# Token-major last down-projection: split weights begin 128 bytes further on in their tile, and the three widened products of a group stand apart

## The chip, the core and the metric

The kernel runs on one core of one Trainium2 chip. The metric is the device time of one execution in microseconds (us); three runs give a median. A profile is one execution with the hardware profiler on; TensorE's granted clock was 0.999 of full speed in it.

## What is computed

A decoder trunk of two layers over 272 tokens (16 learned meta tokens ahead of 256 tokens of input), model width 2048, 16 heads of 128, feed-forward width 8192. Layer 0 is forgetting attention with a squared-ReLU MLP; layer 1 is stick-breaking attention on a shared K and V with a second MLP. The part that the change touches is the end of it:

```python
def squared_relu_mlp(h, w_up, w_down):
    u = h @ w_up
    return jnp.square(jax.nn.relu(u)) @ w_down
...
        h = h + squared_relu_mlp(rms_norm(h, norm_mlp[layer]), w_up[layer], w_down[layer])
    return rms_norm(h, final_norm)[:, N_META:]
```

All values are float32.

## The kernel before

**Products in three.** [...] So each operand is split into a high part and the rest (`hi`, `lo`): ScalarE copies the raw values into the high part, VectorE subtracts it from the raw values. Each product of two matrices becomes three matmuls: hi by hi, lo by hi, hi by lo. Every matmul has its own load of the 128 x 128 stationary operand; the other operand moves through the array, one column per token or per weight.

**Feature-major stages.** Nearly all stages keep the residual stream with features on the partitions and tokens along the row. `gemm_group` (L188) makes 512 output features: the weights are stationary, 128 x 128 at a time, and `x` moves, 272 columns wide in layer 0, 256 columns in layer 1 from its query projection on (`t0` = M = 16, which leaves the meta tokens out), 272 again in the shared K and V. A group has four blocks `kb` of 512 input features, each in two halves (`hf`) of two chunks of 128 (`kc`). One half is a transfer of 512 KB into `raw` on SyncE's queue, one copy on ScalarE (L235) and one subtraction on VectorE (L236), into tiles `whi` and `wlo` that each have four buffers. With `t0` = 0 a chunk's three matmuls stand in a row (L258); with `t0` = 16 the part of the product is the outer loop (L256), so that all hi-by-hi products of a run come first. `gemm_matmul` (L175; its matmul is L177 in the profile) pins the order of the products on TensorE.

**Where operands begin.** A tile of split weights has rows of two chunks, each 576 floats (2304 bytes) wide, of which 512 are used. With `t0` = 16 these begin at float 16 of 576, 64 bytes behind the chunk's beginning; with `t0` = 0 the chunks lie packed, 512 floats each, from 0 on. The tiles of `x` (`Split`, L105) have 16 rows of 640 floats (2560 bytes); `ROWS` places the two parts in a row: `hi` at float 48 and `lo` at 368 with `t0` = 0 (192 and 1472 bytes), at 0 and 320 with `t0` = 16 (0 and 1280 bytes). The pool of the split weights and that of the `x` tiles are opened one behind the other, and all these tiles are whole multiples of 256 bytes long.

**Widened products.** In some groups with `t0` = 16 a few products take `SPAN` = 6 columns more than the 256 that are needed (262). The six columns go into the part of the accumulator's bank that nobody reads. `widen` names the chunks for which the product of the group's first 128 outputs is widened, in each of its three parts.

**The last quarter.** The last of the four down-projections of layer 1 (`last_down`, L835) runs token-major: tokens are on the partitions of the result, so that the final norm and the output need no transpose. Here `x` (the tile `x_u`) is stationary, 128 tokens `b` at a time, and the split weights move, 256 columns `h` at a time. `load_split` (L269) fetches and splits a block as above (L275, L283, L284); `token_products` (L288, its matmul is L293) issues for each entry `(kc, b, h)` of an order the three matmuls in a row, and `behind` (L183) pins each one behind the last. Four groups `g` of 512 outputs have 4 blocks x 4 chunks x 2 x 2 x 3 = 192 matmuls each, 768 in all. In groups 0 to 2, blocks 0 to 2 go through the order kc, b, h, and block 3 finishes one accumulator after the other, each followed by `add_rows` (L799). In group 3 tokens `b` = 0 go through all blocks first (96 matmuls) and `finish_rows` (L813) sends them out, while `b` = 1 goes through the same weights a second time; so all four blocks must be kept, and blocks 1 and 2 lie in `home`, a tile in an `x` buffer with the same rows of 576 floats. The split weights' 512 floats begin at float 16 here too (L282). With `widen` set, the three matmuls of the group's first entry (block 0, chunk 0, b = h = 0) are 262 columns wide (L291).

Of the kernel before, what the change touches and what calls it, by code (L numbers as in the profile page):

```python
# [27 lines left out]
SPAN = 6  # L28
# [8 lines left out]
def yoco_kernel(ctx: ExitStack, tc: tile.TileContext, hT_in, gains, b_f, w_f, w_qkv0, w_o0, w_up, w_dn,  # L37
# [145 lines left out]
    def behind(ins):  # L183

        tc.add_manual_dep(ins.ins, queued[0].name, mybir.DependencyInfo(mybir.DependencyClass.NoSync,
                                                                        mybir.DependencyReason.DATA))
# [82 lines left out]
    def load_split(wblk, kb, label, home=None):  # L269

        src_w = wblk[kb].rearrange("p (k c) -> p k c", k=4)
        parts = []
        for hf in range(2):
            raw = wraw.tile([P, 2, 512], F32, tag="raw", name=f"raw_{label}_{kb}_{hf}")
            nc.sync.dma_start(raw, src_w[:, 2 * hf:2 * hf + 2])  # L275
            if home is None:
                hi = wspl.tile([P, 2 * 576], F32R, tag="whi", name=f"whi_{label}_{kb}_{hf}").rearrange(
                    "p (k c) -> p k c", k=2)
                lo = wspl.tile([P, 2, 576], F32R, tag="wlo", name=f"wlo_{label}_{kb}_{hf}")
            else:  # L280
                hi, lo = home[:, hf, 0], home[:, hf, 1]
            hi, lo = hi[:, :, 16:528], lo[:, :, 16:528]  # L282
            nc.scalar.activation(hi, raw, AF.Copy)  # L283
            nc.vector.tensor_tensor(out=lo, in0=raw, in1=hi.bitcast(F32), op=ALU.subtract)  # L284
            parts.append((hi, lo))
        return parts

    def token_products(accs, sp, parts, kb, order, widen=False):  # L288

        for kc, b, h in order:  # L290
            over = SPAN if widen and kb == kc == b == h == 0 else 0  # L291
            for w, x in ((0, sp.hi), (1, sp.hi), (0, sp.lo)):
                ins = nc.tensor.matmul(accs[b][h][:, :256 + over], x[:, 4 * kb + kc, b * P:(b + 1) * P],  # L293
                                       parts[kc // 2][w][:, kc % 2, 256 * h:256 * h + 256 + over],
                                       start=kb == kc == w == 0 and x is sp.hi, stop=kb == kc == 3 and x is sp.lo)
                behind(ins)
                queued[:] = [ins.ins]
# [243 lines left out]
    for g in range(4):  # L541
# [44 lines left out]
        for j in range(4):  # L586
            h = 4 * g + j
# [247 lines left out]
    def last_down(f, u):  # L835
# [3 lines left out]
        for g in range(4):  # L839
            pool, tag = ((patt, "patt"), (pacc, "acc"))[g % 2]  # L840
            accs = [[pool.tile([P, 512], F32, tag=tag, name=f"acc_t{g}_{b}_{h}") for h in range(2)] for b in range(2)]
            parts = []
            for kb in range(4):
                parts.append(load_split(w_dn[1, f, g], kb, f"t{g}", home[:, kb - 1] if g == 3 and kb in (1, 2) else None))
                if g == 3:
                    token_products(accs, u, parts[kb], kb, [(kc, 0, h) for kc in range(4) for h in range(2)], True)
                elif kb < 3:
                    token_products(accs, u, parts[kb], kb, [(kc, b, h) for kc in range(4) for b in range(2)
                                                            for h in range(2)], True)
                else:  # L850
                    for b in range(2):
                        for h in range(2):
                            token_products(accs, u, parts[kb], kb, [(kc, b, h) for kc in range(4)])
                            add_rows(g, b, h, accs[b][h])
# [68 lines left out]
```

## Time and profile before

| What | us |
| --- | --- |
| median of three runs | 2263.16 |
| lowest and highest of them | 2263.07, 2263.64 |
| profiled execution | 2263.8 |
| its span (first to last instruction) | 2262.1 |
| around the span | 1.7 |
| last quarter on TensorE (L293), first to last start | 2163.8 to 2254.2 |

PE is TensorE's matmuls, PEld its weight loads, DVE VectorE, ACT ScalarE, POOL GpSimd, SP SyncE. A row of one line's instructions has the tiles (out<-in), the count, the least, median and greatest time of one in ns, the first and last start in us, and the shapes. A matmul's time is longer than the distance to the next one, because matmuls are pipelined; the pace of a stretch is the distance of its first and last start over the count less one. Rows of the timeline have start, duration and what is done; neighbouring instructions with the same tiles are merged, with their count and the shape of the first.

### The profile page before, as it was taken

How to read it: one execution, taken by the hardware profiler on the slowest of the kernel's cores; microseconds unless marked ns; L12 is line 12 of the kernel's file. 1: busy time of each engine (PE TensorE's matmuls, PEld its weight loads, DVE VectorE, ACT ScalarE, POOL GpSimd, SP SyncE). 2: the span in 40 equal slices, each digit the busy share in tenths (PEclk: the TensorE clock that was granted, in tenths of full speed). 3: DMA queues.
4: the chain of work that ended last, by engine and by line, in shares of the span. 5: the costliest groups of instructions: out<-in, count | busy, mean ns of one | idle time of the engine just before them, and what ended most of it. 6: DMA issues, size and time to landing. Idle time of an engine off the chain costs nothing.

```text
span 2262.1 us, 44965 instructions
## 1 busy us (share of the span) xinstructions
PE 2253.3 (100%) x18845; PEld 2251.0 (100%) x18845; DVE 1390.2 (61%) x1997; ACT 1125.4 (50%) x1577; POOL 114.8 (5%) x220
## 2 busy tenths in 40 slices
PE   9999999999999999999999999999999999999998
PEld 9999999999999999999999999999999999999998
DVE  7877786554455455455566688876555555555654
ACT  6664565453354344344454577755544443543543
POOL 1000000000000000000000011100000000001421
PEclk9999999999999999999999999999999999999999
DMA  7545545555555555555555544565655656556564
GB/s 248 184 153 178 184 161 169 186 169 185 179 176 182 174 177 185 173 184 177 170 192 183 179 163 159 172 202 186 201 188 190 205 187 201 189 190 204 188 193 144
DMA packets 116507, 413.37 MB, mean 183 GB/s; under 512 B 13456, under 2 KB 15776, under 8 KB 116304
## 3 DMA queue, kind: packets, MB, share of 16 engines
q1 hardware_dynamic: 113904, 406.25, 55.1%
q10 hardware_dynamic: 2000, 3.03, 0.5%
q8 instruction: 147, 2.41, 0.4%
q0 software_dynamic: 400, 1.21, 0.1%
q14 instruction: 56, 0.46, 0.1%
HBM read 408.33 MB, written 2.11 MB: 181 GB/s over the span
## 4 chain that ended last, share of the span: by engine, by line
PE 100%; DVE 0%; ACT 0%; issue 0%; DVEq 0%
PE acc L177 93%; PE acc_t L293 4%; PE ps L400 1%; PE po L495 1%; PE ps L398 0%; PE po L498 0%; PE idle L68 0%; PE pf L344 0%; PE pc L486 0%; PE pom L641 0%; PE ps L605 0%; DVE hrow L832 0%; DVE hrow L830 0%; PE pf_sum L351 0%; DVE hrow L803 0%; DVE sqr L806 0%
## 5 line engine op out<-in xcount | busy, mean ns | idle before, releaser
L236 DVE TENSOR_TENSOR wlo<-raw,whi 128x1024 fp32r<-128x1024 f32 (+1 forms) x742 | 890.7, 1217 | 604.4 <-ACT whi L235 598.1
L235 ACT ACTIVATE whi<-raw 128x1024 fp32r<-128x1024 f32 (+1 forms) x742 | 764.3, 1050 | 881.8 <-PE acc L177 850.6
L177 PE MATMUL acc<-x_m,whi 128*128 128x272 f32 (+1 forms) x4096 | 642.6, 281 | 0.0
L177 PE MATMUL acc<-x_u,whi 128*128 128x272 f32 (+1 forms) x3584 | 576.7, 282 | 0.0
L177 PEld LDWEIGHTS acc<-x_m,whi 128*128 128x128 f32 x4096 | 565.6, 188 | 0.0
L177 PEld LDWEIGHTS acc<-x_u,whi 128*128 128x128 f32 x3584 | 504.0, 188 | 0.0
L177 PE MATMUL acc<-x_m,wlo 128*128 128x272 f32 (+1 forms) x2048 | 441.0, 281 | 0.0
L177 PE MATMUL acc<-x_u,wlo 128*128 128x272 f32 (+1 forms) x1792 | 404.1, 282 | 0.0
L177 PE MATMUL acc<-x_a,whi 128*128 128x272 f32 (+1 forms) x2048 | 352.9, 286 | 0.0
L177 PEld LDWEIGHTS acc<-x_m,wlo 128*128 128x128 f32 x2048 | 323.3, 188 | 0.0
L177 PEld LDWEIGHTS acc<-x_a,whi 128*128 128x128 f32 x2048 | 300.5, 189 | 0.9 <-issue 0.5
L177 PEld LDWEIGHTS acc<-x_u,wlo 128*128 128x128 f32 x1792 | 290.7, 188 | 0.0
L177 PE MATMUL acc<-x_a,wlo 128*128 128x272 f32 (+1 forms) x1024 | 252.8, 285 | 0.0
L177 PE MATMUL acc<-x_kv,whi 128*128 128x272 f32 x1024 | 192.4, 287 | 0.0
L177 PEld LDWEIGHTS acc<-x_a,wlo 128*128 128x128 f32 x1024 | 175.7, 189 | 0.0
L177 PE MATMUL acc<-x_o,whi 128*128 128x272 f32 (+2 forms) x1024 | 161.9, 282 | 0.0
L177 PEld LDWEIGHTS acc<-x_kv,whi 128*128 128x128 f32 x1024 | 160.2, 188 | 0.0
L177 PE MATMUL acc<-x_kv,wlo 128*128 128x272 f32 x512 | 147.2, 288 | 0.0
L177 PEld LDWEIGHTS acc<-x_o,whi 128*128 128x128 f32 x1024 | 141.8, 188 | 0.0
L177 PE MATMUL acc<-x_o,wlo 128*128 128x272 f32 (+1 forms) x512 | 110.3, 282 | 0.0
L300 DVE TENSOR_TENSOR rows<-acc,rows 128x272 f32<-128x272 f32 (+1 forms) x144 | 62.2, 432 | 74.2 <-PE acc L177 74.2
L177 PEld LDWEIGHTS acc<-x_kv,wlo 128*128 128x128 f32 x512 | 96.5, 188 | 0.0
(216 smaller groups left out, 1529.2 us busy)
## 6 DMA issues: line engine op xcount, KB each, us to landing
raw<-w_up SPq DMA_DIRECT2D x256, 512.0 KB, 3.8
raw<-w_dn SPq DMA_DIRECT2D x224, 512.0 KB, 3.7
raw<-w_qkv SPq DMA_DIRECT2D x92, 512.0 KB, 4.0
raw<-w_o SPq DMA_DIRECT2D x64, 512.0 KB, 4.3
raw<-w_kv SPq DMA_DIRECT2D x64, 512.0 KB, 3.7
raw<-w_q SPq DMA_DIRECT2D x32, 512.0 KB, 4.4
raw_t<-w_dn SPq DMA_DIRECT2D x32, 512.0 KB, 4.3
fk<-f_dram ACTq DMA_DIRECT2D x4, 544.0 KB, 7.9
```

The source lines that it names most:

```text
L177: ins = nc.tensor.matmul(*args, **kw).ins
L235: on_act = nc.scalar.activation(hp, src, AF.Copy)
L236: on_dve = nc.vector.tensor_tensor(out=lp, in0=src, in1=hp.bitcast(F32), op=ALU.subtract)
L293: ins = nc.tensor.matmul(accs[b][h][:, :256 + over], x[:, 4 * kb + kc, b * P:(b + 1) * P], parts[kc // 2][w][:, kc % 2, 256 * h:256 * h + ...
L300: nc.vector.tensor_tensor(out=hT[:, c, t0:], in0=acc, in1=hT[:, c, t0:], op=ALU.add)
L400: nc.tensor.matmul(ps[:, 144:416], qs[a][:, j, :], ks[b][:, j, :], start=i == 0, stop=i == 2)
L495: ins = nc.tensor.matmul(po[:, i, :], vk, pk, start=i == k == 0, stop=False)
```

## The change

Two edits. In `load_split` the 512 used floats of each chunk begin at float 48 instead of 16 of 576, that is 192 instead of 64 bytes behind the chunk's beginning; this holds for `whi`, `wlo` and `home`, and for what ScalarE and VectorE write and TensorE reads. In `token_products` the widened products of a group are no longer the three matmuls of the first entry, but the first matmul (hi by hi) of the entries 0, 2 and 4 of block 0's order: the 1st, the 7th and the 13th. In groups 0 to 2 these are chunk 0 with b = 0, chunk 0 with b = 1 and chunk 1 with b = 0; in group 3 they are chunks 0, 1 and 2 with b = 0; h is 0 in all. Nothing else is touched.

```diff
-            hi, lo = hi[:, :, 16:528], lo[:, :, 16:528]
+            hi, lo = hi[:, :, 48:560], lo[:, :, 48:560]
             nc.scalar.activation(hi, raw, AF.Copy)
             nc.vector.tensor_tensor(out=lo, in0=raw, in1=hi.bitcast(F32), op=ALU.subtract)
             parts.append((hi, lo))
...
-        for kc, b, h in order:
-            over = SPAN if widen and kb == kc == b == h == 0 else 0
+        for i, (kc, b, h) in enumerate(order):
             for w, x in ((0, sp.hi), (1, sp.hi), (0, sp.lo)):
+                over = SPAN if widen and kb == w == 0 and x is sp.hi and i in (0, 2, 4) else 0
                 ins = nc.tensor.matmul(accs[b][h][:, :256 + over], x[:, 4 * kb + kc, b * P:(b + 1) * P],
                                        parts[kc // 2][w][:, kc % 2, 256 * h:256 * h + 256 + over],
                                        start=kb == kc == w == 0 and x is sp.hi, stop=kb == kc == 3 and x is sp.lo)
```

## The prediction

> **What bounds the kernel now.** I read the page's busy table first, then the chain that ended last, then the instructions of single lines.
>
> ```profile
> span 2262.1 us, 44965 instructions
> PE 2253.3 (100%) x18845; PEld 2251.0 (100%) x18845; DVE 1390.2 (61%) x1997; ACT 1125.4 (50%) x1577; POOL 114.8 (5%) x220
> PE 100%; DVE 0%; ACT 0%; issue 0%; DVEq 0%
> PE acc L177 93%; PE acc_t L293 4%; PE ps L400 1%; PE po L495 1%; PE ps L398 0%; PE po L498 0%; PE idle L68 0%; PE pf L344 0%; PE pc L486 0%; PE pom L641 0%; PE ps L605 0%; DVE hrow L832 0%; DVE hrow L830 0%; PE pf_sum L351 0%; DVE hrow L803 0%; DVE sqr L806 0%
> ```
>
> TensorE is the whole chain; L293, the only matmul that the diff touches, is 4% of it. Nothing but the start-to-start time of TensorE's products can carry a gain there. So I asked for the instructions of L293, and for the same number of products of L177 directly before it: the last up-projection of layer 1, also 256 columns wide.
>
> ```profile
> L177 PE MATMUL acc<-x_m,whi x511: 275/276/280, 2076.8 to 2163.2; 128*128 128x256 f32 x170, 128*128 128x262 f32 x1
> L177 PE MATMUL acc<-x_m,wlo x256: 275/276/279, 2077.6 to 2163.7; 128*128 128x256 f32 x126, 128*128 128x262 f32 x2
> ...
> L293 PE MATMUL acc_t<-whi_t,x_u x448: 278/279/287, 2163.8 to 2254.2; 128*128 128x256 f32 x147, 128*128 128x262 f32 x3
> L293 PE MATMUL acc_t<-wlo_t,x_u x224: 278/280/286, 2163.9 to 2254.1; 128*128 128x256 f32 x108, 128*128 128x262 f32 x4
> L293 PE MATMUL acc_t<-home,x_u x96: 279/279/281, 2234.5 to 2251.4; 128*128 128x256 f32 x96
> its engine sat idle before it (us, times) until:
> ```
>
> Each row has the count, the least/median/greatest time of one in ns, and the first and last start. L177: 511 + 256 = 767 products, 2076.8 to 2163.7, so 86.9 / 766 = **113.4 ns** from start to start. L293: 448 + 224 + 96 = 768 products, 2163.8 to 2254.2, so 90.4 / 767 = **117.9 ns**. No releaser stands under L293's "sat idle" line: TensorE waits for no data in either stretch, each product has the same width and its own weight load, and yet each costs 4.4 ns more. The time of one tells the two paces apart too: median 276 ns against 279 to 280.
>
> **What differs between the two.** From the code: the product's moving operand and the next product's weight load are both read from SBUF. The pools lie one behind another, and the split tiles (4608 bytes each, 18 x 256) and the x tile's rows (2560 bytes, 10 x 256) keep one remainder by 256. So I count starts from each tile's own beginning, modulo 256. L177 in layer 1: x moves from 0, weights are loaded from 64; moving minus loaded is -64, that is 192. L293: weights move from 64, x is loaded from 0; the difference is 64. The change makes it 192. Layer 0 has 192 too (x at 192, weights at 0), in the order that L293 uses (three products of one chunk in a row), at 272 columns:
>
> ```profile
> L177 PE MATMUL acc<-x_u,whi x512: 285/287/289, 506.1 to 600.6; 128*128 128x272 f32 x171
> L177 PE MATMUL acc<-x_u,wlo x256: 284/287/289, 506.4 to 600.7; 128*128 128x272 f32 x128
> ```
>
> 768 products in 94.6 us, 123.3 ns each; scaled by 256/272 that is 116.1 ns.
>
> The pace is also a state that outlasts its cause. In layer 1's first output-projection group, difference 192, a transpose is put between products; the rows before, behind and after it:
>
> ```profile
> L177 PE MATMUL acc<-x_o,whi x8: 276/276/279, 1469.2 to 1470.0; 128*128 128x256 f32 x7, 128*128 128x262 f32 x1
> ...
> L177 PE MATMUL acc<-x_o,whi x8: 280/281/369, 1470.2 to 1471.1; 128*128 128x256 f32 x7, 128*128 128x262 f32 x1
> ...
> L177 PE MATMUL acc<-x_o,wlo x7: 276/276/285, 1471.3 to 1472.0; 128*128 128x256 f32 x7
> ```
>
> ```profile
> 1470.16 0.27 PE L769 MATMUL pvc<-ident,pk_vc 128*128 128x128 f32 x1
> 1470.19 1.19 PE L177 MATMUL acc<-x_o,whi 128*128 128x262 f32 x8
> 1471.22 1.09 PE L177 MATMUL acc<-x_o,wlo 128*128 128x262 f32 x8
> ```
>
> Eight products run with a median of 281 ns until the next 262-column one at 1471.22; behind it they run at 276. So at 192 both paces exist, and a widened product standing alone ended the slow one. At 64 the fast pace does not hold:
>
> ```profile
> 2163.33 0.62 PE L177 MATMUL acc<-x_m,wlo 128*128 128x256 f32 x4
> 2163.79 0.28 PE L293 MATMUL acc_t<-whi_t,x_u 128*128 128x262 f32 x1
> 2163.90 0.28 PE L293 MATMUL acc_t<-wlo_t,x_u 128*128 128x262 f32 x1
> 2164.03 0.40 PE L293 MATMUL acc_t<-whi_t,x_u 128*128 128x262 f32 x2
> 2164.27 0.28 PE L293 MATMUL acc_t<-wlo_t,x_u 128*128 128x256 f32 x1
> ```
>
> TensorE arrives in the fast pace without a gap, (2163.79 - 2163.33) / 4 = 115 ns with the rounding of the starts, and is slow from the second product, (2164.27 - 2163.79) / 4 = 120 ns.
>
> **The change part by part.** Start of the halves: no instruction is added, removed or moved. It takes 768 products from 117.9 ns to some pace between bounds. I take 113.4, the row nearest in width, engine state and difference: 767 x 4.45 ns = **3.4 us**. Toward less, the row nearest in order and difference is layer 0's, scaled: 116.1 ns, 767 x 1.8 = 1.4 us. The bounds are zero on one side and a second stall of the same size on either (rivals). ScalarE's and VectorE's splits write at the new start too; bounded by their rows in layer 0 (start 0) and layer 1 (start 64):
>
> ```profile
> L236 DVE TENSOR_TENSOR wlo<-raw,whi 128x1024 fp32r<-128x1024 f32 x101 | 122.3, 1224 | 120.2 <-ACT whi L235 120.2
> ...
> L235 ACT ACTIVATE whi<-raw 128x1024 fp32r<-128x1024 f32 x102 | 106.2, 1056 | 150.0 <-PE acc L177 149.1 <-ACT sq_a L148 0.8
> ```
>
> ```profile
> L236 DVE TENSOR_TENSOR wlo<-raw,whi 128x1024 fp32r<-128x1024 f32 x111 | 134.3, 1231 | 101.9 <-ACT whi L235 99.8
> ...
> L235 ACT ACTIVATE whi<-raw 128x1024 fp32r<-128x1024 f32 x111 | 114.8, 1058 | 152.1 <-PE acc L177 152.1
> ```
>
> 1224 and 1231 ns, 1056 and 1058 ns: I take zero, and both engines wait on TensorE anyway.
>
> Widened products: three per group before (the three of the first chunk), three after (the first of orders 0, 2 and 4); 12 in all both times, 6 columns each, into accumulator columns that nobody reads. The sum is 0; on either side less than 12 x (120 - 113.4) = 0.08 us. What spacing is worth lies in the state, not in columns.
>
> Cover that shrinks: if TensorE runs ahead, weights must come earlier. The tightest place is the last group's first pass, where each block serves only 24 products.
>
> ```profile
> 2236.46 1.37 DVE L284 TENSOR_TENSOR wlo_t<-raw_t,whi_t 128x1024 fp32r<-128x1024 f32 x1
> ...
> 2237.82 1.70 DVE L284 TENSOR_TENSOR wlo_t<-raw_t,whi_t 128x1024 fp32r<-128x1024 f32 x1
> ```
>
> The last split ends at 2239.5. Block 3 starts behind home's last product there, product 72 of the pass; its second half is needed 12 products on, product 84 of the group and 576 + 84 = 660 of the stretch: 2163.8 + 660 x 0.1179 = 2241.6. Slack 2.1 us. At 113.4 ns TensorE is there 660 x 4.45 = 2.9 us earlier. How the splits move with it:
>
> ```profile
> 2217.73 1.06 ACT L283 ACTIVATE whi_t<-raw_t 128x1024 fp32r<-128x1024 f32 x1 [1.77 <-PE acc_t L293]
> 2220.56 1.06 ACT L283 ACTIVATE whi_t<-raw_t 128x1024 fp32r<-128x1024 f32 x1 [1.76 <-PE acc_t L293]
> 2224.41 1.06 ACT L283 ACTIVATE home<-raw_t 128x1024 fp32r<-128x1024 f32 x1 [2.79 <-DMA raw_t<-w_dn]
> ```
>
> Up to 2220.6 TensorE releases them (the last field); from 2224.4 they wait for transfers, whose buffers those splits free. At 2217.7, (2217.7 - 2163.8) / 0.1179 = 457 products in, TensorE is 457 x 4.45 ns = 2.0 us ahead, and the transfers with it: 1.2 us of slack stay. If nothing moved, TensorE would wait 0.8 us once.
>
> The tail behind the last product (2254.2 to 2262.1) is VectorE, ScalarE and the output's transfer in series; it moves as a whole.
>
> **Sum.** Profiled execution 2263.8 us (span 2262.1, 1.7 around it): 2263.8 - 3.4 = 2260.4, span 2258.7. The three runs' median is 2263.16, 0.64 lower, so 2263.16 - 3.4 = **2259.8 us**, 0.15% less.
>
> [...]
>
> **The rivals.**
> A, no change (2262.9 to 2263.5): the slow pace belongs to the token-major order or to x being the loaded side. For: the slow spell at 1470 exists at 192 as well; L293 is slow in all four groups. Against: layer 0 has the same order, and its scaled pace is lower than L293's.
> B, part of it (2260.4 to 2262.8): layer 0's scaled pace, 2263.16 - 1.4 = 2261.8, or the fast pace in two groups of four, 2261.5. For: the state can be lost, as at 1470.
> C, slower: with weights moving from 192 each product meets one more stall in place of one less, of the size that separates the paces, 4.45 ns: 122.3 ns, 2266.6 us. The entry's 120 ns shows that slower products occur. It is 0.2% only from 4.5 us / 767 = 5.9 ns per product, 123.8 ns; two such stalls (8.9 ns) give 2270.0.
> D, faster still: one more stall of 4.45 ns goes, 109.0 ns, 2 x 3.4 = 6.8 us, 2256.4. Against: no 256-column stretch of the trace runs below 113.4.
> [...]
>
> **How the numbers follow.** Forecast (2259.4 to 2260.2) 0.62, A 0.17, B 0.13, C 0.05, D 0.03. The range runs from 2259.4 to 2263.3: forecast, B and most of A. A measurement of this kernel tells about 0.2% (4.5 us) from no change; the forecast, A, B and the first step of C are all inside that. Faster by more: D, 0.03. Slower by more: the far part of C, 0.02. Within: 0.95.
>
> **What would show it.** Right: L293's median falls to 276 ns, first to last start to about 87.0 us, span to 2258.7, no releaser under its "sat idle" line, the splits' times unchanged. A: 279 to 280 ns and 90.4 us. B: 276 in some groups, or 277 to 278 throughout. C: above 283. A wait of L293 on VectorE in the last group's first pass would mean that the slack was misjudged.

## The result, and the profile after

The kernel after takes 2260.23 us (median of 22 runs, 2259.36 to 2262.72), the kernel before beside it 2263.51 us (22 runs, 2262.80 to 2265.59): 3.3 us less, ratio 0.9985, 95% interval 0.9979 to 0.9992. The forecast was 2259.8 us, 3.4 us less. The profiled execution of after took 2261.43 us, its span 2259.7.

First the same view as before: line L293's matmuls on TensorE in the kernel after (count, least/median/greatest ns of one, first and last start in us).

```profile
L293 PE MATMUL acc_t<-whi_t,x_u x448: 276/276/286, 2164.5 to 2251.8; 128*128 128x256 f32 x146, 128*128 128x262 f32 x4
L293 PE MATMUL acc_t<-wlo_t,x_u x224: 276/276/384, 2164.6 to 2251.7; 128*128 128x256 f32 x112
L293 PE MATMUL acc_t<-home,x_u x96: 276/276/276, 2232.9 to 2249.1; 128*128 128x256 f32 x96
```

Two things are to be seen. The median fell from 279 or 280 ns to 276 ns in all three rows, the figure that L177 had all along. And 2164.5 to 2251.8 is 87.3 us where it was 90.4: 3.1 us less, a pace of 87.3 / 767 = 113.8 ns. The greatest time of the second row, 384 ns, is new. The waits of the last quarter's middle (who waited for whom; us in total, times, longest) tell why:

```profile
...
DVE home L284 <- ACT home L283: 2.3, 1, 2.3
ACT home L283 <- DMA raw_t<-w_dn: 0.5, 1, 0.5
PEld acc_t L293 <- DVE wlo_t L284: 0.2, 1, 0.2
```

Once, in the last group, TensorE's weight load waited for a split on VectorE, 0.2 us. The timeline shows its place: 0.39 us between two starts that are 0.23 apart elsewhere, then one product of 0.38, and within a few products the fast pace again.

```profile
2231.02 0.28 PE L293 MATMUL acc_t<-wlo_t,x_u 128*128 128x256 f32 x1
2231.14 0.39 PE L293 MATMUL acc_t<-whi_t,x_u 128*128 128x256 f32 x2
2231.53 0.38 PE L293 MATMUL acc_t<-wlo_t,x_u 128*128 128x256 f32 x1
2231.75 0.41 PE L293 MATMUL acc_t<-whi_t,x_u 128*128 128x256 f32 x2
2231.99 0.28 PE L293 MATMUL acc_t<-wlo_t,x_u 128*128 128x256 f32 x1
2232.10 0.39 PE L293 MATMUL acc_t<-whi_t,x_u 128*128 128x256 f32 x2
2232.33 0.28 PE L293 MATMUL acc_t<-wlo_t,x_u 128*128 128x256 f32 x1
```

The rest of the program did not change its pace. L177's last up-projection stretch in the kernel after, to be held against the rows of before:

```profile
L177 PE MATMUL acc<-x_m,whi x511: 276/276/279, 2077.6 to 2164.0; 128*128 128x256 f32 x170, 128*128 128x262 f32 x1
L177 PE MATMUL acc<-x_m,wlo x255: 276/276/279, 2078.4 to 2164.3; 128*128 128x256 f32 x126, 128*128 128x262 f32 x2
```

766 products in 86.7 us, 113.3 ns. L293 begins at 2164.5 us instead of 2163.8: this execution lost 0.7 us earlier. The first 30 us and the 1139 us behind them, before and then after (length, then busy time and count of PE, PEld, DVE, ACT and POOL, granted clock, DMA share, GB/s), put that in the start, where the first weights arrive: in the first 30 us TensorE has 206 products instead of 214 and is busy 28.52 us instead of 28.89, while in the long rest its count and busy time are the same.

```profile
0.00:30.00 30.00, 28.89 (x214) 28.75 (x218) 24.57 (x48) 24.27 (x48) 7.56 (x25) 1.00 0.88 299
30.00:1169.00 1139.00, 1139.00 (x9249) 1137.20 (x9250) 679.94 (x1027) 543.13 (x784) 20.23 (x41) 1.00 0.54 177
```

```profile
0.00:30.00 30.00, 28.52 (x206) 27.84 (x207) 23.39 (x47) 22.65 (x44) 7.34 (x25) 1.00 0.85 289
30.00:1169.00 1139.00, 1139.00 (x9249) 1137.05 (x9249) 681.22 (x1027) 544.25 (x787) 20.23 (x41) 1.00 0.54 177
```

So the span fell by 2.4 us: 3.1 less in L293, 0.7 more ahead of it. Over the experiments that change nothing ahead of the last quarter's tiles L293 begins anywhere from 2162.9 to 2164.8 us, so a single execution's total is a poor measure of a change of 3 us. L293's own first and last start measure it better, and the experiments are read by them.

### The profile page after: what moved, and what is told of

Same layout as the page of the kernel before. It is cut to its first block, busy times and chain, and to the rows that moved or that the text cites. A ratio compares the mean times of both kernels' runs of the same rounds, so it can differ in the third digit from the quotient of the medians.

```text
span 2259.7 us, 44965 instructions
## 1 busy us (share of the span) xinstructions
PE 2250.6 (100%) x18845; PEld 2247.4 (99%) x18845; DVE 1390.7 (62%) x1997; ACT 1125.6 (50%) x1577; POOL 112.4 (5%) x220
## 4 chain that ended last, share of the span: by engine, by line
PE 99%; DMA 1%; DVE 0%; ACT 0%; issue 0%; DVEq 0%; ACTq 0%
PE acc L177 93%; PE acc_t L293 4%; DMA raw<-w_qkv 1%; PE ps L400 1%; PE po L495 1%; PE ps L398 0%; PE po L498 0%; DMA rows<-hT_in 0%; PE pf L344 0%; DVE wlo L236 0%; PE pc L486 0%; DVE x_a L132 0%; DVE ssq_a L149 0%; ACT x_a L131 0%; ACT whi L235 0%; PE ps L605 0%
## 5 line engine op out<-in xcount | busy, mean ns | idle before, releaser
L177 PE MATMUL acc<-x_m,whi 128*128 128x272 f32 (+1 forms) x4096 | 642.6, 281 | 0.0
L177 PE MATMUL acc<-x_u,whi 128*128 128x272 f32 (+1 forms) x3584 | 576.6, 282 | 0.0
L177 PEld LDWEIGHTS acc<-x_m,whi 128*128 128x128 f32 x4096 | 565.7, 188 | 0.0
L177 PEld LDWEIGHTS acc<-x_u,whi 128*128 128x128 f32 x3584 | 504.0, 188 | 0.0
L177 PE MATMUL acc<-x_m,wlo 128*128 128x272 f32 (+1 forms) x2048 | 440.7, 281 | 0.0
L177 PE MATMUL acc<-x_u,wlo 128*128 128x272 f32 (+1 forms) x1792 | 403.9, 282 | 0.0
L177 PE MATMUL acc<-x_a,whi 128*128 128x272 f32 (+1 forms) x2048 | 352.8, 285 | 0.1
L177 PEld LDWEIGHTS acc<-x_m,wlo 128*128 128x128 f32 x2048 | 323.2, 188 | 0.0
L177 PEld LDWEIGHTS acc<-x_a,whi 128*128 128x128 f32 x2048 | 300.2, 188 | 1.3 <-issue 0.9
L177 PEld LDWEIGHTS acc<-x_u,wlo 128*128 128x128 f32 x1792 | 290.7, 188 | 0.0
L177 PE MATMUL acc<-x_a,wlo 128*128 128x272 f32 (+1 forms) x1024 | 252.8, 285 | 0.3 <-DVE wlo L236 0.3
L177 PE MATMUL acc<-x_kv,whi 128*128 128x272 f32 x1024 | 192.4, 287 | 0.0
L177 PEld LDWEIGHTS acc<-x_a,wlo 128*128 128x128 f32 x1024 | 175.6, 188 | 0.7 <-DVE wlo L236 0.7
L177 PE MATMUL acc<-x_o,whi 128*128 128x272 f32 (+2 forms) x1024 | 162.0, 282 | 0.0
L177 PEld LDWEIGHTS acc<-x_kv,whi 128*128 128x128 f32 x1024 | 160.0, 188 | 0.0
L177 PE MATMUL acc<-x_kv,wlo 128*128 128x272 f32 x512 | 147.1, 287 | 0.0
L177 PEld LDWEIGHTS acc<-x_o,whi 128*128 128x128 f32 x1024 | 141.8, 188 | 0.0
L177 PE MATMUL acc<-x_o,wlo 128*128 128x272 f32 (+1 forms) x512 | 110.2, 281 | 0.0
L177 PEld LDWEIGHTS acc<-x_kv,wlo 128*128 128x128 f32 x512 | 96.4, 188 | 0.0
```

Source lines behind the costliest of these rows:

```text
L177: ins = nc.tensor.matmul(*args, **kw).ins
```

## The experiments

**The theory**: L293's pace is set by where the moving operand begins relative to where the stationary operand is loaded from (in bytes, modulo 256, from the beginnings of their tiles; called the difference from here on), and at a difference of 192 a fast pace exists. **The rivals**: the spacing of the widened products does it; the moving operand's own start does it; any start but 64 does it.

All diffs are against the kernel after. Every pace and every time of one below is read from the profile of the run it stands with. Where no ratio is given, an experiment is one profiled execution. Six executions at the fast pace without a wait took 87.0 to 87.1 us from L293's first to its last start, and three at difference 64 took 90.4 us, so differences of a few tenths can be read.

**The two edits apart.** First the start alone, the widened products together again:

```diff
-                over = SPAN if widen and kb == w == 0 and x is sp.hi and i in (0, 2, 4) else 0
+                over = SPAN if widen and i == kb == 0 else 0
```

> The split weights begin at 192 as in the kernel after, the three widened products stay together in the group's first entry as before. Theory (the difference of moving start and loaded start, modulo 256, sets the pace, 192 being a fast one): L293 runs at 113.4 ns, median 276 ns, first to last start about 87.1 us, about 3.3 us less than the kernel before. Rival (the spacing of the widened products ends the slow pace, as at 1470 us in the profile before): L293 stays at 117.8 ns and 279 ns, 90.4 us, the time within 0.5 us of before.

```profile
L293 PE MATMUL acc_t<-whi_t,x_u x448: 276/276/285, 2163.5 to 2250.5; 128*128 128x256 f32 x147, 128*128 128x262 f32 x3
L293 PE MATMUL acc_t<-wlo_t,x_u x224: 276/276/282, 2163.6 to 2250.4; 128*128 128x256 f32 x108, 128*128 128x262 f32 x4
```

276 ns and 87.0 us; 2260.13 us (10 runs), ratio 0.9985 (0.9976 to 0.9995). The start alone gives all of the change's gain; standing apart adds nothing that shows. Then the spacing alone, the start put back:

```diff
-            hi, lo = hi[:, :, 48:560], lo[:, :, 48:560]
+            hi, lo = hi[:, :, 16:528], lo[:, :, 16:528]
```

> The widened products stand apart as after, the split weights begin at 64 as before. Theory of the difference: slow as before, L293 at 117.8 ns, 279 to 280 ns, 90.4 us. Rival of the spacing: 113.4 ns, 276 ns, 87.1 us.

```profile
L293 PE MATMUL acc_t<-whi_t,x_u x448: 279/280/283, 2162.9 to 2253.3; 128*128 128x256 f32 x146, 128*128 128x262 f32 x4
```

280 ns, 90.4 us; 2263.59 us (10 runs), ratio 0.9999 (0.9989 to 1.0008). The spacing alone gives nothing. The rival of the spacing falls.

**Does it need widened products at all?** Start at 192, none widened:

```diff
-                over = SPAN if widen and kb == w == 0 and x is sp.hi and i in (0, 2, 4) else 0
+                over = 0
```

> The split weights begin at 192, and no product of the last quarter is widened (256 columns throughout). The run with the three together had the fast pace from its 9th product on, so: theory (the difference alone makes the fast pace; the state finds it by itself): 276 ns, 113.4 ns, first to last start 86.9 to 87.1 us. Rival (a widened product is needed to end the slow state with which the stretch begins): L293 at 117 to 118 ns, 279 to 280 ns and about 90.3 us, in the first group at least.

```profile
L293 PE MATMUL acc_t<-whi_t,x_u x448: 279/281/283, 2163.3 to 2253.6; 128*128 128x256 f32 x150
L293 PE MATMUL acc_t<-wlo_t,x_u x224: 281/281/283, 2163.4 to 2253.5; 128*128 128x256 f32 x112
L293 PE MATMUL acc_t<-home,x_u x96: 281/281/282, 2234.0 to 2250.8; 128*128 128x256 f32 x96
```

281 ns, 90.3 us: slow from end to end, no better than before (117.7 ns). My theory in its plain form, that the difference alone makes the pace, falls here. At 192 there are two paces, 113.4 ns in the run with the start alone and 117.7 here, and without a product of another width the stretch keeps the longer one for all of its 768 products. In this stretch the gain needs both: the difference 192 **and** some widened product, whichever way it stands.

Elsewhere a widened product isn't always needed. In the kernel before, the query projection (L177, difference 192) begins directly behind 272-column products; its first widened product comes at 1191.2 us, and ahead of it the median is 276 ns already:

```profile
L177 PE MATMUL acc<-x_a,whi x123: 275/276/279, 1169.8 to 1190.6; 128*128 128x256 f32 x123
L177 PE MATMUL acc<-x_a,wlo x62: 275/276/280, 1170.1 to 1190.9; 128*128 128x256 f32 x62
```

Nor does every product of another width lead to 276 ns: the transpose at 1470 us in the prediction has 128 columns, and 281 ns followed it. Which disturbance leads to which pace stays open.

**How long does one push hold?** The widened products in group 0 only:

```diff
-                                                            for h in range(2)], True)
+                                                            for h in range(2)], g == 0)
```

(and `True` left out in the call of group 3)

> The kernel after, with the three widened products in group 0 of the last quarter only; groups 1 to 3 have 256 columns throughout. Theory (at difference 192 the fast pace is a state that holds by itself once a widened product has led into it): 276 ns and 113.4 ns in all four groups, first to last start 87.0 us. Rival (each group's new accumulators need a widened product again): 117.8 ns from group 1 or from some later point on, up to 89.5 us.

```profile
L293 PE MATMUL acc_t<-whi_t,x_u x448: 275/276/285, 2163.1 to 2250.1; 128*128 128x256 f32 x149, 128*128 128x262 f32 x1
L293 PE MATMUL acc_t<-home,x_u x96: 276/276/277, 2231.1 to 2247.3; 128*128 128x256 f32 x96
```

87.0 us, and the home rows of the last group, 588 products and more behind the last widened one (the 13th of 768), are at 276 ns: the three widened products lead into the pace, and it then holds by itself. The first of the three was enough to bring it about. These are the fourth to the sixth product of the stretch in the kernel after, ahead of its second widened product, the seventh:

```profile
L293 PE MATMUL acc_t<-whi_t,x_u x2: 276/278/279, 2164.9 to 2165.1; 128*128 128x256 f32 x2
L293 PE MATMUL acc_t<-wlo_t,x_u x1: 277/277/277, 2165.0 to 2165.0; 128*128 128x256 f32 x1
```

They come down to 276 ns, where the run without widened products stands at 281. Whether the pace would hold to the end behind the first alone was not run.

**Difference, or the operand's own start?** The weights back at 64, and instead the last quarter's `x` 128 bytes later, so that the difference is 192 with the moving operand where it was:

```diff
-            hi, lo = ROWS[t0]
+            hi, lo = (32, 352) if label == "u1_3" else ROWS[t0]
...
-            hi, lo = hi[:, :, 48:560], lo[:, :, 48:560]
+            hi, lo = hi[:, :, 16:528], lo[:, :, 16:528]
```

> The split weights begin at 64 as before, but the tile of x that L293 loads as its stationary operand begins 128 bytes later in its rows (floats 32 and 352 instead of 0 and 320), so the difference of moving start and loaded start is 64 - 128 = 192 modulo 256, with the moving operand where it was. Widened products apart as after. Theory of the difference: fast, 276 ns, 113.4 ns, 87.1 us. Rival (the moving start alone matters): slow, 279 to 280 ns, 117.8 ns, 90.4 us.

```profile
L293 PE MATMUL acc_t<-whi_t,x_u x448: 276/276/280, 2163.0 to 2250.0; 128*128 128x256 f32 x146, 128*128 128x262 f32 x4
```

Fast: 276 ns, 87.0 us. The plain difference is 64 - 128 = -64 here and 192 - 0 = 192 in the kernel after; both are at 276 ns, so counting modulo 256 held for this pair. And the counter-test, both operands moved by 128 bytes, difference 64 again (the first of these two edits alone):

> The kernel after (weights from 192, widened products apart) with the stationary x of the last quarter 128 bytes later too, so the difference is 192 - 128 = 64 again while both operands begin elsewhere than before. Theory of the difference: slow, 117.8 ns, median 279 to 280 ns, 90.4 us, the time of the kernel before. Rival (a moving start of 192, or an x at 128, is what makes it fast): 113.4 ns, 276 ns, 87.0 us.

```profile
L293 PE MATMUL acc_t<-whi_t,x_u x448: 276/280/283, 2164.7 to 2255.1; 128*128 128x256 f32 x146, 128*128 128x262 f32 x4
```

Slow: 280 ns, 90.4 us, with the weights where the kernel after has them. The rival of the moving start falls in both directions; what counts, given widened products, is the difference.

**Other differences.**

```diff
-            hi, lo = hi[:, :, 48:560], lo[:, :, 48:560]
+            hi, lo = hi[:, :, 0:512], lo[:, :, 0:512]
```

and in the same way 32:544 and 56:568.

> The split weights begin at 0, so the difference is 0; widened products apart as after. Theory of the difference: a pace other than that of 192 is possible; as the two reads then begin in the same place, the slow 117.8 ns (279 to 280 ns, 90.4 us) or worse. Rival (any start other than 64 will do): 113.4 ns, 276 ns, 87.1 us.

> The split weights begin at 128, difference 128, widened products apart as after. So far 0 gave 120.0 ns, 64 gave 117.8, 192 gave 113.3. If the pace falls with the difference over the whole 256: between 113.3 and 117.8 ns, about 115.5, 88.6 us. If there are but steps of whole stalls: either 113.3 (87.1 us) or 117.8 (90.4 us).

> The split weights begin at 224, difference 224, half-way from 192 (113.3 ns) to 256, which is 0 again (120.0 ns). Theory of the difference modulo 256: a pace between the two, 113.3 to 120.0 ns, that is 87.0 to 92.0 us, most likely 116.7 ns, 89.5 us. Rival (any start from 192 on is fast, no period of 256): 113.3 ns, 87.0 us.

Two rows of each, in this order; the `home` rows are 256 columns wide throughout:

```profile
L293 PE MATMUL acc_t<-whi_t,x_u x448: 278/283/286, 2163.9 to 2255.8; 128*128 128x256 f32 x146, 128*128 128x262 f32 x4
L293 PE MATMUL acc_t<-home,x_u x96: 283/283/283, 2235.8 to 2252.9; 128*128 128x256 f32 x96
```

```profile
L293 PE MATMUL acc_t<-whi_t,x_u x448: 274/281/289, 2163.1 to 2254.2; 128*128 128x256 f32 x146, 128*128 128x262 f32 x4
L293 PE MATMUL acc_t<-home,x_u x96: 279/281/285, 2234.4 to 2251.3; 128*128 128x256 f32 x96
```

```profile
L293 PE MATMUL acc_t<-whi_t,x_u x448: 276/281/286, 2163.3 to 2254.1; 128*128 128x256 f32 x146, 128*128 128x262 f32 x4
L293 PE MATMUL acc_t<-home,x_u x96: 277/280/285, 2234.3 to 2251.2; 128*128 128x256 f32 x96
```

| difference | widened | median ns | first to last start | pace |
| --- | --- | --- | --- | --- |
| 0 | apart | 283 | 91.9 us | 119.8 ns |
| 64 (before) | together, apart | 279 to 280 | 90.4 | 117.9 |
| 128 | apart | 281 | 91.1 | 118.8 |
| 192 (after without its one wait) | together, apart, group 0 only | 276 | 87.0 | 113.4 |
| 192 | none | 281 | 90.3 | 117.7 |
| 224 | apart | 281 | 90.8 | 118.4 |

The table's paces are over the whole of L293; the 120.0, 117.8 and 113.3 ns of the expectations at 0, 64 and 192 lie within 0.2 ns of them. The pace does not fall evenly with the difference, which was one expectation for 128, nor is everything from 192 on fast, which was the rival for 224. Of the five differences tried, 192 alone has the 113.4 ns pace; 0 is worst, as the expectation for it allowed. At 128 and 224 single products keep differing: 279 to 285 and 277 to 285 ns in the `home` rows, against 283 throughout at 0 and 276 at 192. At 128 neither expectation came true. At 224 the pace lies in the expected range, but 1.7 ns above the most likely value (116.7).

**The one wait.** The last group's order of splits on ScalarE, in the kernel after (the field in brackets is the idle time before, and what ended it):

```profile
2223.07 1.06 ACT L283 ACTIVATE home<-raw_t 128x1024 fp32r<-128x1024 f32 x1 [2.81 <-DMA raw_t<-w_dn]
2224.04 1.04 ACT L283 ACTIVATE whi_t<-raw_t 128x1024 fp32r<-128x1024 f32 x1
2227.69 1.06 ACT L283 ACTIVATE home<-raw_t 128x1024 fp32r<-128x1024 f32 x1 [2.61 <-DMA raw_t<-w_dn]
2228.65 1.05 ACT L283 ACTIVATE whi_t<-raw_t 128x1024 fp32r<-128x1024 f32 x1
```

`whi_t` at 2228.65 is block 0's second half; it stands behind block 1's `home`, which waited 2.61 us for its transfer. VectorE's part stands behind block 1's `home` and an addition of `add_rows`, and ends at 2231.48, where TensorE needed it at 2231.4:

```profile
2229.92 0.42 DVE L803 TENSOR_TENSOR hrow<-acc_t,hrow 128x256 f32<-128x256 f32 x1
2230.26 1.22 DVE L284 TENSOR_TENSOR wlo_t<-raw_t,whi_t 128x1024 fp32r<-128x1024 f32 x1
```

In the run with the start alone the same step waited 0.65 us:

```profile
2222.28 1.06 ACT L283 ACTIVATE home<-raw_t 128x1024 fp32r<-128x1024 f32 x1 [3.08 <-DMA raw_t<-w_dn]
2223.25 1.04 ACT L283 ACTIVATE whi_t<-raw_t 128x1024 fp32r<-128x1024 f32 x1
2224.94 1.06 ACT L283 ACTIVATE home<-raw_t 128x1024 fp32r<-128x1024 f32 x1 [0.65 <-DMA raw_t<-w_dn]
```

To take the place away, not the transfer, the extra tile holds blocks 0 and 1 instead of 1 and 2:

```diff
-                parts.append(load_split(w_dn[1, f, g], kb, f"t{g}", home[:, kb - 1] if g == 3 and kb in (1, 2) else None))
+                parts.append(load_split(w_dn[1, f, g], kb, f"t{g}", home[:, kb] if g == 3 and kb < 2 else None))
```

> The kernel after with the weights of the last group's blocks 0 and 1 in the extra tile instead of blocks 1 and 2, so that no split of block 0 stands behind a split that waits for a later transfer. Theory (the one wait of TensorE in the profile after, some 0.28 us in the last group's first pass, came from block 0's second half being split behind block 1's transfer): no wait of L293's weight loads on VectorE, first to last start 87.0 us, the time 0 to 0.3 us under the kernel after (2260.2). Rival (the wait is the late landing of a transfer in that one execution): no steady difference from after; the wait may be absent or stand at another block.

```profile
L293 PE MATMUL acc_t<-whi_t,x_u x448: 276/276/285, 2164.8 to 2251.8; 128*128 128x256 f32 x147, 128*128 128x262 f32 x3
L293 PE MATMUL acc_t<-home,x_u x96: 276/276/279, 2230.1 to 2246.4; 128*128 128x256 f32 x93, 128*128 128x262 f32 x3
```

No wait, 87.0 us; 2260.11 us (11 runs), ratio 0.9984 (0.9975 to 0.9993), not to be told from the kernel after. But the runs with the start alone, with `x` moved and with group 0 widened have the order of after, are as fast, and show no such wait either; their `home` split waited 0.65, 0.65 and 1.89 us for the transfer, where after's waited 2.61. So the wait in after's profile is best read as one late landing met by a small slack, the rival's side; whether the other placing helps in the executions where a transfer is late stays open.

**Can layer 0 be pushed too?** It has the difference 192 at 272 columns. The kernel after, with the first chunk's products of every second group of layer 0's MLP widened:

```diff
-            if t0:
+            if t0 or label[0] in "mu":
...
-                           widen=(0,) if t0 == M and g % 2 == 1 else ())
+                           widen=(0,) if g % 2 == 1 else ())
...
-                gemm_group(w_dn[layer, f, g], u, t0, evac, widen=(0,) if t0 == M and g % 2 == 1 else ())
+                gemm_group(w_dn[layer, f, g], u, t0, evac, widen=(0,) if g % 2 == 1 else ())
```

(the first of the three prepares the six columns in layer 0's tiles of the MLP) The second run has, besides,

```diff
-                if t0 or pinned[0] and load_x is not None:
+                if True:
```

> The kernel after, and in layer 0's MLP every second group has three widened products as well (278 instead of 272 columns, the first chunk's). Theory (the 123.3 ns of the 272-column products, difference 192, are a slow state like the one without widened products): their pace falls, by the same 4.4 ns to 119 ns at most, 6144 products of that MLP or some 27 us. Rival (at 272 columns this is the only pace): 123.3 ns as before, the time that of the kernel after, 2260.2.

> As the run before, and the products of all 272-column groups in the order of layer 1 (the part of the product as the outer loop) instead of three of a chunk in a row. If order has a part in the pace at 272 columns: another pace than 123.3 ns. If not: 123.3 ns, 2260.2 us.

Rows of L177 in the stretch from 506.3 to 600.9 us, of the first run and then of the second:

```profile
L177 PE MATMUL acc<-x_u,whi x509: 284/288/296, 506.8 to 600.8; 128*128 128x272 f32 x168, 128*128 128x278 f32 x2
L177 PE MATMUL acc<-x_u,wlo x254: 284/287/291, 507.1 to 600.7; 128*128 128x272 f32 x125, 128*128 128x278 f32 x2
```

```profile
L177 PE MATMUL acc<-x_u,whi x504: 282/288/294, 507.8 to 600.5; 128*128 128x272 f32 x166, 128*128 128x278 f32 x2
L177 PE MATMUL acc<-x_u,wlo x251: 283/287/291, 508.8 to 600.8; 128*128 128x272 f32 x124, 128*128 128x278 f32 x2
```

763 products in 94.0 us and 755 in 93.0 us: 123.4 and 123.3 ns, against 123.3 before. Neither widened products nor the order change the pace at 272 columns; other differences were not tried there. The single times, 2261.40 and 2263.37 us, lie within and above after's runs; the second one's L293 begins only at 2166.7 us. No version was found that beats the kernel after.

## Why the prediction was right, and where it was not

*What bounds it.* Right: nothing moved but the pace of L293's products, and 3.1 us of the stretch's 90.4 went (3.4 in the runs without the wait), which the medians show as 3.3.

*The pace at 192.* The term was 767 x 4.45 ns = 3.4 us, taken from L177's 113.4 ns; measured 113.4 ns and 276 ns, 87.0 us in the runs without the wait (113.8 ns and 87.3 us with it). That the neighbouring stretch in another order and with other roles of weights and `x` would carry over was a choice; layer 0's scaled 116.1 ns, the price of rival B, was the other. No row ahead of the result decided between the two, so that it held is in part luck. Rival B's row was a poor measure: at 272 columns neither widened products nor the order moved the pace from 123.3 ns by more than 0.1.

*The two paces as a state.* Right, but it weighs more than the prediction made of it. The prediction read from the spell at 1470 us that a widened product can end the slow pace, and then priced spacing at nothing; it did not say that without any widened product the gain would be zero. It is: 90.3 us. The forecast came true because both kernels have widened products, a condition it rested on without naming it, and that much is luck. The same run has rival A's number, 117.7 ns at 192, but not its mechanism: order and roles are those of the kernel after, which has 113.4 ns.

*Widened products.* Sum 0: right for their six columns and for standing apart (87.0 us together or apart).

*The rivals C and D.* Neither came about at 192. A pace longer than before's exists at the difference 0, 119.8 ns, though by 1.9 ns and not by the 4.45 of C; one below 113.3 ns, as D has it, showed in no run. The stall of 4.45 ns that both count with was the author's estimate from the two paces of before; no row shows one.

*Splits and tail.* Right but for four splits. The 28 copies into `whi_t` have a median of 1061 ns before and 1062 after, VectorE's 28 subtractions 1226 ns both times; VectorE's four into `home` went from 1226 to 1327 ns. From L293's last start to the end of the span it is 7.9 us in both. VectorE's row in the kernel after:

```profile
L284 DVE TENSOR_TENSOR wlo_t<-raw_t,whi_t x28: 1216/1226/1227, 2156.8 to 2237.2; 128x1024 fp32r<-128x1024 f32 x28
```

*The cover that shrinks.* Here a step failed. It named block 3's second half as the tightest place, with 1.2 us left, and expected no wait. The wait came at block 0's second half, which the step did not look at: its split stands on ScalarE behind a `home` split that waits for a later transfer (2.61 us in the kernel after), so that one transfer's late landing reaches it. Its price, once, was the 0.3 us between 87.3 and 87.0. By the prediction's own sign (a wait of L293 on VectorE in the last group's first pass) the slack was misjudged there; at block 3 the estimate held, since the last split ended at 2238.5 us and TensorE was there at 2239.7, 1.2 us later.

*What the difference is worth.* Ahead of the result the difference of starts stood together with other roles and another order; the runs take it apart. With instructions, order and widths the same, 128 bytes between the two starts are worth 4.4 ns per product: 90.4 us in the kernel before against 87.0 in the run with the start alone, and 90.4 in the run with the spacing alone against 87.0 in the one with `x` moved. No row of the profile tells why, and why 192 is the good difference stays open.

## What to carry to other kernels

Where two stretches of matmuls with the same width and no waits have different times of one, compare where their moving and stationary operands begin, relative to each other, and try several starts: of five differences one helped here. Rows that are padded already make that free, as here. Measure the pace by first and last start of the line, not by a single total: those of the kernel after spread over 3.4 us. And look for a pace that outlasts its cause: an edit that is useless alone (here the start without a widened product) can be the half of one that works.

## What the runs showed of the hardware that was not expected

At the same difference of 192 a stretch of 256-column products ran at 113.4 ns or at 117.7 ns to its end, decided by products of 262 columns at its beginning, of which the first alone brought the time of one down to 276 ns by the sixth product. With three of them in the first group the lower pace then held over the 755 products of one width behind them. It came back within a few products after TensorE's one wait, with no widened product behind the wait (one stood directly ahead of it). Of the differences 0, 64, 128, 192 and 224 only 192 reached the lower pace, with 0 the slowest at 119.8 ns. At 272 columns the pace was 123.3 to 123.4 ns in two orders, with and without widened products.
